# Lambda and the first gate group's rows moved into the input projections of a hybrid attention step

## Chip, cores and metric

One NeuronCore of one Trainium2 chip runs the whole step as one program. The metric is device time in microseconds; several runs are shown by their median. The change is told from no change when it moves the median by more than about 0.5%, which is 13 us here.

## What is computed

One layer for 2048 prompt frames of one stream and 16 new frames of each of 8 running streams (2176 rows in all, width 1024):

```
h   = rms_norm(x, g_in)
qa, ka, va, z_a, qd, ckv, kpe, z_b, m_a, m_b = split(h @ w_in)
lam = exp(sum(lq1*lk1)) - exp(sum(lq2*lk2)) + lam_init
o_a = (softmax(q1 k1) - lam * softmax(q2 k2)) v          # differential attention, 4 heads
o_b = latent attention over rms_norm(ckv) and rope(kpe)    # 4 heads
y_a = W_oa(rms_norm(o_a) * silu(z_a));  y_b = W_ob(o_b * silu(z_b))
out = x + W_out(sigmoid(m_a) * y_a + sigmoid(m_b) * y_b)
```

A final norm follows. `m_a` and `m_b` together are 2048 columns of `w_in`: 16 blocks of 128, called gates here.

## The kernel before

Every matmul of the layer is done in float32 split in two: a value becomes a high part `hi` (a cast on ACT) and a low part `lo` (a subtraction on DVE), and a product is three matmuls, hi·hi, hi·lo and lo·hi (`_mm3`, L97).

The program runs in phases, built by `build` (L1364):

- `_phase_a` (L129): the input projections except the gates, in three parts of rows (`PARTS`), each part 11 pairs of output blocks. Pairs that get a rotation (`rope_pair`, L354) load cosine and sine into the tile `cs`, of which there are two buffers (L360). The normalised rows stand split in `X` (L160); two of these tiles, tags `hi0` and `lo0`, come from the outer pool `zh`.
- `_phase_a2` (L468): queries, keys and values of the latent branch, in six groups of 384 rows (the last has 256). Its results go to DRAM through three rotating buffers (`pair`, L496).
- `_phase_b` (L1006): attention over the prompt, 64 blocks (8 per head and branch; names `d` for differential, `m` for latent). It starts with `_lam` (L660): a product of the four lambda vectors on DVE, one small matmul, an exponential on ACT, two small DVE steps that leave the tile `nlam`.
- `_gates` (L423): the gate columns, in six groups of rows. For one group: the rows are loaded again (four tiles `zx` of two blocks each, from the outer pool `zs`, tag `st`, two buffers), scaled by the norm (L441) and split into `z_hi` and `z_lo` (L442, L443; one buffer each, in the place of `hi0` and `lo0`). Then 16 units follow: load the weight block `zs` (512 KB, the same two `st` buffers), split it into two `zw` tiles (four buffers in all), 24 matmuls of 384 columns into the one PSUM buffer of `zp`, a tanh on ACT (`zt`, L464) and a store to DRAM. Group 1 also writes its split weights to DRAM (`wz`, L458); groups 2 and 5 read these and split nothing.
- `_sample` and `_phase_c`: attention of the 8 running streams, and the output projections.

The order of the instructions is not the order of the code. A scheduler at build time places every instruction on its engine by priority and by its own estimate of when things are ready; groups 0, 1, 2 and 5 of the gates are given the priority of the end of phase A (`prio`, L1374) although their code stands behind phase B, so that their matmuls go wherever TensorE would wait. The engines then run their own lists strictly in order, and the DMA issues of the whole kernel stand in one list, SP's. What the scheduler decided is fixed in the program; on the chip an instruction whose input is late holds up everything behind it on its engine.

Names in the rows: the trace leaves out numbers, so `z` is any gate unit; in the order lists `z1_4` is unit 4 of group 1, `zx0_2` the third row tile of group 0, `zs1_0` a weight block, `sd0_0_...` scores of differential head 0, block 0.

Of the kernel before, what the change touches and what calls it, by code (L numbers as in the profile page):

```python
# [20 lines left out]
P = 128  # L21
# [25 lines left out]
def _consts(c, pool):  # L47
    nc = c.nc
    c.ident = pool.tile([P, P], F32, name="ident")
    make_identity(nc, c.ident)  # L50
    c.ones = pool.tile([P, P], F32, name="ones")
    nc.gpsimd.memset(c.ones, 1.0)
    c.mhalf = pool.tile([P, 64], F32, name="mhalf")
    nc.gpsimd.memset(c.mhalf, -0.5)
    c.vec = pool.tile([P, 20], F32, name="vec")
    nc.sync.dma_start(c.vec, c.i["vec"])
    c.g_in = c.vec[:, 0:8]
    c.g_qa = c.vec[:, 8:12]
    c.g_kva = c.vec[:, 12:14]
    c.gsub = pool.tile([P, 1], F32, name="gsub")  # L60
    nc.vector.tensor_scalar(c.gsub, c.vec[:, 14:15], 1.0 - LAM_INIT, None, op0=ALU.mult)
    c.maskq = pool.tile([P, P], BF16, name="maskq")
    nc.gpsimd.memset(c.maskq, 0.0)
    nc.gpsimd.memset(c.maskq[0:1, 0:64], 1.0)
    c.maskk = pool.tile([P, 64], BF16, name="maskk")
    nc.gpsimd.memset(c.maskk, 0.0)
    nc.gpsimd.memset(c.maskk[0:1, :], NEG)
# [61 lines left out]
def _phase_a(c):  # L129

    nc, tc = c.nc, c.tc
    with (
# [91 lines left out]
        def last_sum(p, raw):  # L224

            n = PARTS[p][1]
            for j in range(4):
                split(raw[j, 1, 0], (z[:, j, n : 2 * n] for z in X[0]))
# [179 lines left out]
        for p in range(len(PARTS)):  # L408
            raw = load_part(p)
            sums(p, raw)  # L410
            v_block(p)
            kpe_block(p)
            last_sum(p, raw)
            for i, f in enumerate(pairs(p)):
                f()
                if p + 1 < len(PARTS):
                    if i < 2 * PARTS[p + 1][1] // P:
                        squares(p + 1, i)
                    elif i == 6:
                        factors(p + 1)  # L420


def _gates(c, prio, g, after, ready):  # L423

    nc, tc = c.nc, c.tc

    def ahead():
        return tc.high_priority(offset=tc.cur_priority - prio)

    t0, n = GROUPS[g]  # L430
    with ahead():
        R = c.zh.tile([P, NG], F32, tag="R", name=f"Rz{g}")[:, :n]
        nc.sync.dma_start(R, c.Rh[:, t0 : t0 + n])
        hi = c.zh.tile([P, KT, NG], F32R, tag="hi0", name=f"z_hi{g}")[:, :, :n]
        lo = c.zh.tile([P, KT, NG], F32R, tag="lo0", name=f"z_lo{g}")[:, :, :n]
        for k2 in range(4):
            x = c.zs.tile([P, 2, NG], F32, tag="st", name=f"zx{g}_{k2}")[:, :, :n]
            nc.sync.dma_start(x, c.i["xT"][:, 2 * k2 : 2 * k2 + 2, t0 : t0 + n])
            for j in range(2):
                k = 2 * k2 + j  # L440
                nc.vector.scalar_tensor_tensor(x[:, j], x[:, j], c.g_in[:, k : k + 1], R, op0=ALU.mult, op1=ALU.mult)  # L441
                nc.scalar.copy(hi[:, k], x[:, j])  # L442
                nc.vector.tensor_tensor(lo[:, k], x[:, j], hi[:, k].bitcast(F32), op=ALU.subtract)  # L443
    for u in range(16):
        nm = f"{g}_{u}"
        with ahead():
            w = [c.zw.tile([P, KT, P], F32R, tag="w", name=f"zw{l}_{nm}") for l in range(2)]
            if ready:
                for l in range(2):
                    nc.sync.dma_start(w[l].bitcast(F32), c.wz[u, l])  # L450
            else:
                st = c.zs.tile([P, KT, P], F32, tag="st", name=f"zs{nm}")
                nc.sync.dma_start(st, c.i["wu"][22 + u])
                for k in range(0, KT, 4):
                    _split(nc, w[0][:, k : k + 4], w[1][:, k : k + 4], st[:, k : k + 4])
                if g == 1:
                    for l in range(2):
                        nc.sync.dma_start(c.wz[u, l], w[l].bitcast(F32))  # L458
        ps = c.zp.tile([P, 512], F32, tag="z", name=f"z{nm}")[:, :n]
        with tc.issue_after(after) if after else nullcontext():  # L460
            _mm3(nc, ps, [(w[0][:, k], w[1][:, k], hi[:, k], lo[:, k]) for k in range(KT)])
        with ahead():
            s = c.zt.tile([P, NG], F32, tag="t", name=f"zt{nm}")[:, :n]
            nc.scalar.activation(s, ps, AF.Tanh, scale=0.5)  # L464
            nc.sync.dma_start(c.smT[u][:, t0 : t0 + n], s)
# [194 lines left out]
def _lam(c, pool, psum):  # L660
# [5 lines left out]
    nc.tensor.matmul(ps[:, 0:2], c.ones, pr, start=True, stop=True)  # L666
    ex = pool.tile([P, 2], F32, name="lam_ex")
    nc.scalar.activation(ex, ps[:, 0:2], AF.Exp)
    c.nlam = pool.tile([P, 1], F32, name="nlam")
    nc.vector.tensor_tensor(c.nlam, ex[:, 1:2], ex[:, 0:1], op=ALU.subtract)  # L670
    nc.vector.tensor_scalar(c.nlam, c.nlam, -LAM_INIT, None, op0=ALU.add)

# [333 lines left out]
def _phase_b(c):  # L1006
    nc, tc = c.nc, c.tc
    GQ = 256
    with (
# [9 lines left out]
        def bank(tag, name):  # L1019
            return pp.tile([P, 512], F32, tag=tag, name=name, bufs={"s": 4, "pt": 2, "o": 1}[tag])  # L1020

        _lam(c, p1, lambda n: bank("o", n))
        onesr = p1.tile([P, 32], F32R, name="onesr")
        nc.scalar.copy(onesr, c.ones[:, :32])
        kp = p1.tile([P, SEQ], F32R, name="kp")
# [338 lines left out]
def build(tc, ins, outs, upto="z", dump=None):  # L1364
# [3 lines left out]
    with tc.tile_pool(name="const", bufs=1) as pool, tc.tile_pool(name="dram", bufs=1, space=DRAM) as dpool:  # L1368
        _consts(c, pool)
        _scratch(c, dpool)  # L1370
        with ExitStack() as stack:
# [3 lines left out]
            _phase_a2(c)  # L1375
            _phase_b(c)
            for g in (0, 1, 2, 5):
                _gates(c, prio, g, None, g in (2, 5))
            _sample(c, stack)
            for g in (3, 4):  # L1380
                _gates(c, prio, g, c.mm.ins, False)
# [95 lines left out]
```

## Time and profile before

| | us |
|---|---|
| three runs: lowest, median, highest | 2585.27, 2591.4, 2596.58 |
| the profiled execution's own time | 2595.66 |
| its span, first to last instruction | 2593.9 |

| engine | busy us | share of the span |
|---|---|---|
| PE (TensorE matmuls) | 2418.1 | 93% |
| DVE (VectorE) | 1645.4 | 63% |
| ACT (ScalarE) | 1224.7 | 47% |
| POOL (GpSimd) | 470.4 | 18% |

The mean granted TensorE clock is 0.975 of full speed. Busy time is a sum over phases with different limits, and a matmul's end is modelled, so short waits of PE do not show in it. The timeline view gives each instruction's start and length, and in brackets the idle time before it and what ended that idle time. SPq rows are DMA issues, not the transfers.

### The profile page before, as it was taken

The numbers are of one execution on the slowest core, as the hardware profiler recorded it, in microseconds if no ns is written. First come the engines' busy times: TensorE is split into PE (matmuls) and PEld (weight loads), VectorE is DVE, ScalarE is ACT, GpSimd is POOL, SyncE is SP. The second block draws the span as 40 slices with busy tenths as digits, with TensorE's granted clock in tenths as the row PEclk, the third lists the DMA queues.
The fourth block names the chain that finished last, engine by engine and source line by source line (L and its number), as shares of the span: only waits on it lengthen the run. The fifth ranks groups of instructions, "written<-read, shape, count | busy, mean of one in ns | idle before, by whom it ended". The sixth has DMA issues, their size and how long they took to land. (4 is left out here: it accounts for less than half of the span.)

```text
span 2593.9 us, 44001 instructions
## 1 busy us (share of the span) xinstructions
PE 2418.1 (93%) x15426; PEld 2149.4 (83%) x15426; DVE 1645.4 (63%) x3668; ACT 1224.7 (47%) x3042; POOL 470.4 (18%) x730
## 2 busy tenths in 40 slices
PE   6998999997899699999999988998999997999998
PEld 5998999997888689899888977887676674988887
DVE  7897686886676477877776688894333223534334
ACT  5544544543444366766665566783334333311111
POOL 0000000000000032333343234443000002122211
PEclk9999999999899899999999999999999998999999
DMA  6977677686687986574666755316869594544332
GB/s 236 306 268 251 210 252 265 204 280 185 228 277 255 299 285 201 183 227 140 182 194 207 232 170 166 92 58 232 325 254 370 222 380 138 174 128 126 121 115 96
DMA packets 303997, 553.28 MB, mean 213 GB/s; under 512 B 29184, under 2 KB 230176, under 8 KB 288544
## 3 DMA queue, kind: packets, MB, share of 16 engines
q1 hardware_dynamic: 303776, 550.46, 64.0%
q8 instruction: 123, 2.02, 0.3%
q14 instruction: 98, 0.80, 0.1%
HBM read 397.16 MB, written 153.19 MB: 212 GB/s over the span
## 5 line engine op out<-in xcount | busy, mean ns | idle before, releaser
L100 PE MATMUL z<-z_hi,zw 128*128 128x384 f32 (+1 forms) x768 | 264.7, 345 | 47.1 <-ACT zt L464 28.2
L102 PE MATMUL z<-z_hi,zw 128*128 128x384 f32 (+1 forms) x768 | 257.9, 336 | 0.4 <-DVE zw L115 0.4
L101 PE MATMUL z<-z_lo,zw 128*128 128x384 f32 (+1 forms) x768 | 258.1, 336 | 0.1
L1079 ACT ACTIVATE ed<-sd,pmd 128x512 f32<-128x512 f32 (+3 forms) x320 | 201.1, 632 | 43.6 <-DVE pmd L1077 23.0
L1077 DVE TENSOR_REDUCE pmd<-sd 128x1 f32<-128x512 f32 (+3 forms) x320 | 189.4, 603 | 49.9 <-PE sd L1178 30.6
L1178 PE MATMUL sd<-k,q 128*128 128x512 f32 (+2 forms) x640 | 193.1, 391 | 13.3 <-ACT ed L1079 8.9
L100 PEld LDWEIGHTS z<-z_hi,zw 128*128 128x128 f32 x768 | 148.6, 193 | 68.6 <-ACT zt L464 36.1
L1118 POOL TENSOR_SCALAR ed<-ed,ad 128x512 f32<-128x512 f32 (+3 forms) x160 | 115.5, 737 | 317.5 <-DVE ad L1094 142.5
L101 PEld LDWEIGHTS z<-z_lo,zw 128*128 128x128 f32 x768 | 148.8, 194 | 7.3 <-issue 4.1
L102 PEld LDWEIGHTS z<-z_hi,zw 128*128 128x128 f32 x768 | 147.9, 193 | 6.5 <-issue 3.4
L109 POOL TENSOR_SCALAR ss<-ss 128x3 f32<-128x3 f32 (+3 forms) x15 | 3.2, 213 | 792.4 <-DVE ss L529 474.1
L115 DVE TENSOR_TENSOR zw<-zs,zw 128x512 fp32r<-128x512 f32 x128 | 84.4, 688 | 92.9 <-ACT zw L114 90.8
L100 PE MATMUL y<-o,wh_ab 128*128 128x384 f32 (+1 forms) x384 | 127.8, 333 | 13.7 <-DVE sm L1303 10.5
L1118 POOL TENSOR_SCALAR em<-em,am 128x512 f32<-128x512 f32 (+3 forms) x160 | 102.9, 660 | 185.5 <-DVE am L1094 115.5
L101 PE MATMUL y<-o,wh_ab 128*128 128x384 f32 (+1 forms) x384 | 126.6, 330 | 0.0
L102 PE MATMUL y<-o,wl_ab 128*128 128x384 f32 (+1 forms) x384 | 126.3, 329 | 0.0
L1178 PEld LDWEIGHTS sd<-k,q 128*128 128x128 f32 x640 | 105.4, 194 | 23.6 <-ACT ed L1079 15.5
L1079 ACT ACTIVATE em<-sm,pmm 128x512 f32<-128x512 f32 (+3 forms) x160 | 100.2, 629 | 47.0 <-DVE pmm L1077 34.2
L1303 DVE SCALAR_TENSOR_TENSOR sm<-sm,y 128x384 f32<-128x384 f32 (+1 forms) x96 | 50.4, 530 | 112.9 <-PE y L102 111.4
L1308 ACT ACTIVATE m<-sm 128x384 fp32r<-128x384 f32 (+1 forms) x48 | 24.3, 506 | 199.0 <-POOL sm L1306 199.0
L1077 DVE TENSOR_REDUCE pmm<-sm 128x1 f32<-128x512 f32 (+3 forms) x160 | 95.6, 603 | 35.3 <-PE sm L1225 27.4
L1135 ACT CAST pthd<-ptd 128x512 fp32r<-128x512 f32 (+3 forms) x160 | 82.6, 522 | 72.1 <-PE ptd L1132 69.6
(521 smaller groups left out, 7579.3 us busy)
## 6 DMA issues: line engine op xcount, KB each, us to landing
zs<-in_wu_dram SPq DMA_DIRECT2D x64, 512.0 KB
zw<-wz SPq DMA_DIRECT2D x64, 512.0 KB
ksd<-in_ckT_dram SPq DMA_DIRECT2D x32, 1024.0 KB
vsd<-in_cv_dram SPq DMA_DIRECT2D x32, 1024.0 KB
q<-Qs SPq DMA_DIRECT2D x128, 128.0 KB
wz<-zw SPq DMA_DIRECT2D x32, 512.0 KB
ksm<-in_cc_dram SPq DMA_DIRECT2D x16, 1024.0 KB
smT<-zt SPq DMA_DIRECT2D x80, 192.0 KB
```

The lines of the kernel that those rows point to most:

```text
L100: nc.tensor.matmul(out, ah, bh, start=(j == 0), stop=False)
L101: nc.tensor.matmul(out, ah, bl, start=False, stop=False)
L102: last = nc.tensor.matmul(out, al, bh, start=False, stop=(j == n - 1))
L109: c.nc.gpsimd.tensor_scalar(ss, ss, scale, EPS, op0=ALU.mult, op1=ALU.add)
L115: nc.vector.tensor_tensor(lo, src, hi.bitcast(F32), op=ALU.subtract)
L1077: nc.vector.tensor_reduce(nm_, ps[:, :w], axis=AX.X, op=ALU.max, negate=True)
L1079: nc.scalar.activation(e[:, :w], ps[:, :w], AF.Exp, bias=nm_, accum_out=l[:, s, i : i + 1])
L1118: nc.gpsimd.tensor_scalar(p, p, a[:, 0, j : j + 1], 1.0, op0=ALU.mult, op1=ALU.mult)
L1135: nc.scalar.copy(hi, v)
L1178: nc.tensor.matmul(ps[:, :n], qs[s][:, j, qc], ks[s].tiles[i][:, :n], start=(j == 0), stop=(j == 1 and not last))
L1303: nc.vector.scalar_tensor_tensor(s, s, 1.0, ps, op0=ALU.add, op1=ALU.mult)
L1308: nc.scalar.mul(z[0], sm[0], 0.5)
```

## The change

Three edits. The lambda steps run in phase A, in part 0, after the block `kpe_block`, with a PSUM bank of phase A; `nlam` moves to the constant pool. The rows of gate group 0 are loaded and split by a new function, `_gate_rows`, called at the end of phase A's code, and their four `zx` tiles come from the two `cs` buffers of the rotation tables instead of the two `st` buffers. The other groups call the same function with the `st` buffers, as before.

```diff
+            if p == 0:
+                _lam(c, pc, bank)
...
+        c.rows = _gate_rows(c, 0, lambda name: pc.tile([P, 2, NG], F32, tag="cs", name=name, bufs=2))
+
+
+def _gate_rows(c, g, get):
...
+    for k2 in range(4):
+        x = get(f"zx{g}_{k2}")[:, :, :n]
+        nc.sync.dma_start(x, c.i["xT"][:, 2 * k2 : 2 * k2 + 2, t0 : t0 + n])
+        for j in range(2):
+            k = 2 * k2 + j
+            nc.vector.scalar_tensor_tensor(x[:, j], x[:, j], c.g_in[:, k : k + 1], R, op0=ALU.mult, op1=ALU.mult)
+            nc.scalar.copy(hi[:, k], x[:, j])
+            nc.vector.tensor_tensor(lo[:, k], x[:, j], hi[:, k].bitcast(F32), op=ALU.subtract)
+    return hi, lo
...
-def _gates(c, prio, g, after, ready):
+def _gates(c, prio, g, after, ready, rows=None):
...
-        for k2 in range(4):
-            x = c.zs.tile([P, 2, NG], F32, tag="st", name=f"zx{g}_{k2}")[:, :, :n]
...
+    if rows is None:
+        with ahead():
+            rows = _gate_rows(c, g, lambda name: c.zs.tile([P, 2, NG], F32, tag="st", name=name))
+    hi, lo = rows
...
-    c.nlam = pool.tile([P, 1], F32, name="nlam")
...
-        _lam(c, p1, lambda n: bank("o", n))
...
-                _gates(c, prio, g, None, g in (2, 5))
+                _gates(c, prio, g, None, g in (2, 5), c.rows if g == 0 else None)
```

Both programs hold the same number of instructions on every engine. What differs is where they stand.

SP's list at the end of phase A. `qdT`, `ckT` and `gzT` are stores of phase A; `ws_uq` and `qd0` are loads of phase A2. Before:

```order
L438 DMA zx0_2_19654<-in_xT_dram 128x2x384
L438 DMA zx0_3_19662<-in_xT_dram 128x2x384
L385 DMA ckT_84<-m1l12_2_6477 128x320
L481 DMA ws_uq0_6606<-in_wuq_dram 128x512
L385 DMA ckT_84<-wl12_2_6480 128x320
L433 DMA Rz1_20246<-Rh_94 128x384
L385 DMA ckT_84<-vl12_2_6478 128x320
L453 DMA zs0_0_19672<-in_wu_dram 128x1024
L385 DMA ckT_84<-u3l12_2_6479 128x320
L481 DMA ws_uq1_6612<-in_wuq_dram 128x512
L453 DMA zs0_1_19708<-in_wu_dram 128x1024
L509 DMA qd0_6656<-qdT_83 128x4x384
```

And of the change, the same stretch:

```order
L386 DMA qdT_84<-u3l10_2_6354 128x320
L467 DMA zs0_2_19744<-in_wu_dram 128x1024
L437 DMA zx0_2_6613<-in_xT_dram 128x2x384
L437 DMA zx0_3_6621<-in_xT_dram 128x2x384
L386 DMA ckT_85<-m1l12_2_6486 128x320
L495 DMA ws_uq0_6651<-in_wuq_dram 128x512
L386 DMA ckT_85<-wl12_2_6489 128x320
L467 DMA zs0_3_19780<-in_wu_dram 128x1024
```

The weight blocks of units 0 and 1 (`zs0_0`, `zs0_1`) now stand 31 and 19 issues earlier, among phase A's last stores; here unit 2's comes ahead of the third and fourth row tiles, which keep their place.

ACT's list at the border of phases A2 and B. `kz5` and `z_hi1` are splits, `onesr` a constant of phase B, `ed0_0` the first exponentials of attention. Before:

```order
L442 CAST z_hi1_20248<-zx1_2_20266 128x384 x2
L1024 CAST onesr_8364<-ones_65 128x32
L442 CAST z_hi1_20248<-zx1_3_20274 128x384 x2
L668 ACT_TABLE_LOAD
L668 ACTIVATE lam_ex_8359<-lam_ps_8357 128x2
L114 CAST zw0_1_0_20282<-zs1_0_20284 128x512 x2
L114 CAST zw0_1_1_20320<-zs1_1_20322 128x512 x2
L464 ACTIVATE zt1_0_20317<-z1_0_20292 128x384
L1079 ACTIVATE ed0_0_0_0_0_8399,ld0_0_0_8389<-sd0_0_0_0_0_8394,pmd0_0_0_8388 128x128
```

And of the change:

```order
L602 CAST kz5_8370<-kp5_8360 64x256
L478 ACTIVATE zt1_9_20659<-z1_9_20634 128x384
L115 CAST zw0_1_11_20700<-zs1_11_20702 128x512 x2
L478 ACTIVATE zt1_10_20697<-z1_10_20672 128x384
L115 CAST zw0_1_12_20738<-zs1_12_20740 128x512 x2
L478 ACTIVATE zt1_11_20735<-z1_11_20710 128x384
L1036 CAST onesr_8400<-ones_65 128x32
L478 ACTIVATE zt1_12_20773<-z1_12_20748 128x384
L115 CAST zw0_1_13_20776<-zs1_13_20778 128x512 x2
L115 CAST zw0_1_14_20814<-zs1_14_20816 128x512 x2
L478 ACTIVATE zt1_13_20811<-z1_13_20786 128x384
L478 ACTIVATE zt1_14_20849<-z1_14_20824 128x384
```

The next two rows of the change are the table load and `ed0_0`. Before, the first exponentials of attention come behind unit 0 of group 1; now behind unit 14. PE's list agrees: ahead of the first score `sd0_0` stood unit 0 alone, now units 0 to 14, of which 0 to 2 and the start of 3 lie among the last matmuls of phase A2, and 4 to 14 follow each other with no other matmul between.

SP's list at the same border, of the change (before, `kp<-Kp` and the first `q` stood ahead of `zs1_0`):

```order
L467 DMA zs1_13_20778<-in_wu_dram 128x1024
L472 DMA wz_96<-zw1_1_11_20701 128x1024
L472 DMA wz_96<-zw0_1_12_20738 128x1024
L479 DMA smT_88<-zt1_11_20735 128x384
L467 DMA zs1_14_20816<-in_wu_dram 128x1024
L472 DMA wz_96<-zw1_1_12_20739 128x1024
L1038 DMA kp_8402<-Kp_92 128x2048
L1066 DMA q0_0_0_8404<-Qs_80 64x2x256
L1067 DMA q0_0_0_8404<-Qs_80 64x2x256
```

The loads for the first attention blocks now stand behind the weight block of unit 14. With 14 units less to spread, the last unit of group 5 on PE moves from block d2_5/m2_2 of attention forward to about d2_2/m2_5.

## Rows read from the trace of the kernel before

**Rows 1.** The page's first part: busy us, share of the span, instructions.

```profile
PE 2418.1 (93%) x15426; PEld 2149.4 (83%) x15426; DVE 1645.4 (63%) x3668; ACT 1224.7 (47%) x3042; POOL 470.4 (18%) x730
```

**Rows 2.** Windows: stretch, length, busy us by engine, PEclk, DMA share, GB/s.

```profile
620.90:640.00 19.10, 7.16 (x27) 6.62 (x28) 11.43 (x21) 8.13 (x14) 0.00 (x0) 0.73 0.88 266
700.00:862.50 162.50, 152.86 (x862) 146.85 (x860) 110.24 (x233) 71.18 (x146) 8.24 (x17) 0.97 0.84 269
862.50:888.00 25.50, 6.85 (x29) 6.41 (x28) 10.61 (x23) 8.99 (x19) 1.27 (x3) 0.60 0.87 266
```

**Rows 3.** Timeline of PE, first gate units: start us, length us, instruction, idle before.

```profile
631.77 0.69 PE L100 MATMUL z<-z_hi,zw 128*128 128x384 f32 x1 [10.89 <-ACT zw L114]
...
649.38 0.44 PE L100 MATMUL z<-z_hi,zw 128*128 128x384 f32 x1 [4.19 <-ACT zt L464]
...
650.05 0.52 PE L100 MATMUL z<-z_hi,zw 128*128 128x384 f32 x1
...
657.04 0.44 PE L100 MATMUL z<-z_hi,zw 128*128 128x384 f32 x1 [0.96 <-ACT zt L464]
...
661.14 0.34 PE L102 MATMUL z<-z_hi,zw 128*128 128x384 f32 x1
665.97 0.69 PE L100 MATMUL z<-z_hi,zw 128*128 128x384 f32 x1 [4.49 <-ACT zt L464]
```

**Rows 4.** Timeline of ACT, DVE and SP, the rows and first weights of group 0.

```profile
615.64 1.76 ACT L442 CAST z_hi<-zx 128x384 fp32r<-128x384 f32 x4 [4.81 <-PE p4l L324]
...
617.24 1.72 SPq L438 DMA_DIRECT2D zx<-in_xT_dram  x2
...
621.07 1.15 DVE L441 SCALAR_TENSOR_TENSOR zx<-zx,vec,Rz 128x384 f32<-128x384 f32 x2 [1.42 <-DMA zx<-in_xT_dram]
...
625.48 0.36 SPq L453 DMA_DIRECT2D zs<-in_wu_dram  x1
...
626.32 1.02 DVE L443 TENSOR_TENSOR z_lo<-zx,z_hi 128x384 fp32r<-128x384 f32 x2
...
631.11 1.14 ACT L114 CAST zw<-zs 128x512 fp32r<-128x512 f32 x2 [5.49 <-DMA zs<-in_wu_dram]
```

**Rows 5.** Timeline at the border of phases A2 and B.

```profile
873.70 1.28 ACT L668 ACT_TABLE_LOAD   x1
...
873.83 0.58 PE L666 MATMUL lam_ps<-lam_pr,ones 128*128 128x2 f32 x2 [11.21 <-DVE lam_pr L664]
874.57 0.53 SPq L453 DMA_DIRECT2D zs<-in_wu_dram  x1
...
881.19 1.14 ACT L114 CAST zw<-zs 128x512 fp32r<-128x512 f32 x2 [6.02 <-DMA zs<-in_wu_dram]
...
881.86 0.69 PE L100 MATMUL z<-z_hi,zw 128*128 128x384 f32 x1 [7.45 <-ACT zw L114]
```

**Rows 6.** Windows of the tanh line alone, by head: length, busy us (count), PEclk, DMA share, GB/s.

```profile
888.00:1152.63 264.63, 9.82 (x20) 0.99 0.73 237
1152.63:1381.68 229.05, 6.71 (x14) 0.99 0.60 180
...
1607.69:1778.46 170.77, 0.00 (x0) 0.96 0.26 76
```

**Rows 7.** Timeline of ACT, the tanh of the first three units of group 1.

```profile
888.02 0.49 ACT L464 ACTIVATE zt<-z 128x384 f32<-128x384 f32 x1 [3.72 <-PE z L102]
...
893.88 0.49 ACT L464 ACTIVATE zt<-z 128x384 f32<-128x384 f32 x1 [1.44 <-PE z L102]
...
900.51 0.49 ACT L464 ACTIVATE zt<-z 128x384 f32<-128x384 f32 x1 [0.22 <-PE z L102]
```

**Rows 8.** Windows, two stretches of the highest transfer rate; columns as in rows 2.

```profile
885.00:890.00 5.00, 5.00 (x33) 4.82 (x33) 1.63 (x7) 1.83 (x8) 0.01 (x1) 0.95 1.07 372
890.00:895.00 5.00, 4.78 (x28) 4.37 (x27) 2.92 (x8) 2.86 (x9) 1.27 (x3) 1.00 1.03 415
```

**Rows 9.** Timeline of PE, first score and first transpose of attention.

```profile
887.82 0.40 PE L1178 MATMUL sd<-k,q 128*128 128x256 f32 x2
...
893.68 0.49 PE L1132 MATMUL ptd<-ident,ed 128*128 128x128 f32 x3
```

More of the change, by code (lines that the diff above doesn't have):

```diff
@@ L61, in _consts @@
     nc.vector.tensor_scalar(c.gsub, c.vec[:, 14:15], 1.0 - LAM_INIT, None, op0=ALU.mult)
+    c.nlam = pool.tile([P, 1], F32, name="nlam")
     c.maskq = pool.tile([P, P], BF16, name="maskq")
@@ L420, in _phase_a @@
                         factors(p + 1)
-def _gates(c, prio, g, after, ready):
+        c.rows = _gate_rows(c, 0, lambda name: pc.tile([P, 2, NG], F32, tag="cs", name=name, bufs=2))
+def _gate_rows(c, g, get):
+    nc = c.nc
+    t0, n = GROUPS[g]
+    R = c.zh.tile([P, NG], F32, tag="R", name=f"Rz{g}")[:, :n]
+    nc.sync.dma_start(R, c.Rh[:, t0 : t0 + n])
+    hi = c.zh.tile([P, KT, NG], F32R, tag="hi0", name=f"z_hi{g}")[:, :, :n]
+    lo = c.zh.tile([P, KT, NG], F32R, tag="lo0", name=f"z_lo{g}")[:, :, :n]
+    for k2 in range(4):
[8 more added lines that the diff above has]
+def _gates(c, prio, g, after, ready, rows=None):
     nc, tc = c.nc, c.tc
@@ L430, in _gates @@
     t0, n = GROUPS[g]
[L431 to L435, printed above, removed]
-        for k2 in range(4):
-            x = c.zs.tile([P, 2, NG], F32, tag="st", name=f"zx{g}_{k2}")[:, :, :n]
[L438 to L443, printed above, removed]
+    if rows is None:
+        with ahead():
+            rows = _gate_rows(c, g, lambda name: c.zs.tile([P, 2, NG], F32, tag="st", name=name))
+    hi, lo = rows
     for u in range(16):
```

## The prediction

> **What bounds the kernel now.** I read the first part of the page first: PE is busy 2418 of 2594 us, no other engine above 63% [rows 1]. So the time is what PE has to do plus what it waits for, and since both programs hold the same instructions, only the waits, the clock and the overlap can change. I then looked, in the windows, for stretches in which PE is idle around the places that the change touches. There are two: at the end of phase A PE works 7.2 of 19.1 us, at the border of A2 and B 6.9 of 25.5 us, while inside A2 it works 153 of 162.5 us [rows 2]. Next comes the timeline of these stretches, to see what each idle time waits for. The first (10.89 us) ends with the cast of a weight block `zw` [rows 3]. Ahead of it ACT, DVE and SP show the row tiles arriving one after the other, and the weight block issued only at 625.48, when a `st` buffer was free [rows 4]. The second is two waits, 11.21 us for lambda's product on DVE and 7.45 us for `zw` again [rows 5]. At the border the weight block was issued at 874.57 and its cast began at 6.62 us after that; so even without lambda unit 0 of group 1 could not have started much before 881 there. Last I read by head what attention costs with and without gate units [rows 6].
>
> **The price of a unit.** The clean one starts at 657.04, its last matmul starts at 661.14: 4.10 us for 23 steps, 0.178 each, so 24 matmuls are 4.28 us, here 4.3. With one PSUM buffer the next unit waits for the tanh: 0.96 us of idle at best, so that units in a row cannot follow closer than 4.44 + 0.96 = 5.4 us [rows 3].
>
> **Part 1, start of the gates after phase A.** Removed: the two `st` buffers no longer carry row tiles, so weight blocks 0 and 1 are loaded during phase A, 31 and 19 issues earlier on SP. Not removed: four row tiles still share two buffers. The third and fourth are issued where they were, at 617.24, and reach DVE at 621.07; the last split seen there is two subtractions from 626.32 to 627.34 [rows 4]. PE could begin with the first rows' products when the last projection ends, 620.9, and finish unit 0 when the last rows are split, with a few matmuls left: about 629. Before, 24 steps from 631.77 under a half clock (0.69 us a matmul, 0.73 granted over the stretch [rows 2, 3]) end at about 638.3, an estimate. That is 9; unit 1 follows at the bank's pace, which gives back part, so I take **−7.5**. Ends: −4, where the clock still falls during the remaining waits, and −10, no more than the idle time itself is 10.9.
>
> **Part 2, the border.** Lambda goes to phase A: DVE's product, PE's 0.58 us, ACT's two steps. DVE and ACT are not the bound in phase A, which I take from their shares [rows 1]; PE's own 0.58 us stays, **+0.6** (0 to 2, the upper end if its wait on DVE shows, since PE's list is strict). The units of group 1 now reach into the tail of A2, so lambda's 11.2 us and `zw`'s 7.45 us both lose their cause: **−18.7**. The near end, −14, leaves room for one late first block of weights in A2 (an idle of 4.19 or 4.49 us, as seen twice at the first gates [rows 3]).
>
> **Part 3, eleven units with nothing between them.** This is what the change adds. Before, PE did units 1 to 14 of group 1 between the products of attention; now 4 to 14 stand alone ahead of the first score. A unit inside attention costs its 4.3 us and no more: head 1 takes 229.05 us with 14 units, of which 12 are full and two of the short last group at 2.9 (256 of 384 columns); less 12 × 4.3 + 2 × 2.9 = 57.4 it is 171.7, and the head without units takes 170.77 [rows 6]. So in leaving attention each unit returns 4.3 us and costs its pace P in the row: 11 × (P − 4.3). P is at least the 5.4 of the bank. The other limit is traffic: a unit of group 1 loads 512 KB, writes 1024 KB of split weights and 192 KB of results, 1.77 MB. At the 372 and 415 GB/s of the busiest stretches [rows 8] that is 4.8 and 4.3 us; at 266, the rate of the border now [rows 2], 6.7 us. The weight blocks of units 4 on have both `st` buffers from the start, so the loads run ahead, and I take P = 5.6, just above the bank's pace: **+14.3**. Ends: 5.4 (+12.1) and 7.0 (+29.7), the upper one between the traffic at 266 GB/s and the 7.7 us from 649.38 to 657.04 at the first gates [rows 3].
>
> **Part 4, the tail of A2.** Units 0 to 2 and the start of 3 run between A2's last matmuls, where DMA is already at a share of 0.84 [rows 2]. Three times 1.77 MB at 372 GB/s are 14 us of transfers that A2's own loads and stores have to share. In 162.5 us at 0.84 the free share is 26 us, so most fits: **+3**, between 0 and 8.
>
> **Part 5, the first softmax.** Before, unit 1 lay between the first score at 887.82 and the first transpose at 893.68, and covered the exponentials [rows 9]. Now nothing of the gates stands there, and the exponential table's 1.28 us load [rows 5] moves onto this chain. The chain is 5.86 us, of which the other scores fill about 1.4 (an estimate: three more of 0.40): **+4.5**, ends 2 and 8. The first attention loads are now issued behind weight block 14, but that block is wanted some 10 us before the first score, so they should be in time.
>
> **Part 6, filler missing later.** The gate units now end three pairs of blocks earlier in the third head. Attention without them is no slower than with them, net of their 4.3 us [rows 6]: **0**.
>
> **The sum.** −7.5 + 0.6 − 18.7 + 14.3 + 3 + 4.5 = −3.8 us. The 1.8 us around the span stay. Against the profiled execution (2595.7) this gives 2591.9; that execution was 4.3 above the median of the runs, so against the median it is 2587.6, **2588**. This is no measurable change: a difference under 0.5%, 13 us, cannot be told from none here. All ends together would reach from −35 to +34, but they do not fall on one side together.
>
> **Rivals.**
> *It gains more than I allow (faster).* The row of units runs at the bank's 5.4, the start gives its full 10, A2's tail costs nothing, the softmax chain 2, and head 0 loses its crowding: now it takes 264.63 us with 19 units [rows 6], 182.9 without them, 11 more than head 1; with most units gone it could give back 9. Sum: −10 + 0.6 − 18.7 + 12.1 + 0 + 2 − 9 = −23, 2568. For it: DMA share 1.00 and above in that head's start [rows 8]. Against: part of head 0's surplus may be the start of attention itself. It decides from 9 us below my sum on.
>
> *The row of units is paced by its weights (slower).* Each unit needs load, split on ACT and DVE, matmuls, and then a write of its split weights ahead of the next loads in SP's one list. Where this chain is not run ahead, units follow at 7.7 and 8.9 us [rows 3] and tanhs of group 1 at 5.86 and 6.63 [rows 7]. At P = 8: 11 × 2.4 = 26.4 above my sum, +22.6, 2614. It is slower than the bound from P = 7.1 on, that is when DMA gives less than 250 GB/s. Against it: the first gates were late because row tiles held the buffers, and at B's start DMA gave 372.
>
> *The rows gain nothing (same).* The two `cs` buffers hold row tiles 2 and 3 back just as the two `st` buffers did, and SP issues them where it did [rows 4]; if PE's first unit must wait for these anyway, the −7.5 is 0 and the sum +3.7, 2595.
>
> *The clock falls in the row of units (slower).* In the trace, matmuls after 0.96 us of idle are still 0.44 and then 0.34 us long, after 4.19 us of idle 0.52, and after 10.89 us 0.69 [rows 3]: only the longer idles go with the half clock, 1.2 GHz, and a row with 1.1 to 1.3 us between units should stay at 2.4 GHz. If instead the clock were low in half of the eleven units, each of these would take twice its 4.28 us of matmuls: 5.5 × 4.28 = 23.5 above my sum, +19.7, 2611. The Trainium skill, "TensorE: Matmul & The Clock Gate", section "A second HAM failure mode: psum-queue depth-cycling", describes this case: short idles between groups of matmuls, as PSUM buffers are cycled, make the clock swing between its two levels. By that rule this rival would hold; the trace so far does not agree with it after 0.96 us.
>
> **Chances and range.** My sum 0.5; gains more 0.2; paced by weights 0.15; rows gain nothing 0.1; clock 0.05. So faster 0.2, same 0.6, slower 0.2. The range runs from 2573, which takes in most of the ends of the start, the tail and head 0, to 2608, which is P = 7.4; 0.1 is left out at each end, the clock's case among it.
>
> **What would show it.** Right: the first gate matmul at about 621 and unit 1 at about 633; no idle of 11 and 7 us at the border; tanhs of units 4 to 14 some 5.6 us apart with a granted clock near 1; the first transpose about 4.5 us of idle after the scores; heads without units at 171 us. Wrong: tanhs over 7 us apart, PE waiting for `zw` between them, an idle of over 4 us before the first score (its loads late), or PE in A2's tail waiting for `qd` loads.

## The result, and the profile after

The changed kernel takes 2606.52 us (median of 5 runs, 2603.97 to 2607.36), the kernel before in the same comparison 2592.12: ratio 1.0054, interval 1.0041 to 1.0067, 14.4 us slower. The forecast was 2588, no measurable change. The profiled execution of the changed kernel has a span of 2605.6 us, with PE busy for 2440.1 us of it (94%).

At the two places that I had looked at, the long idle times are gone, as forecast. Timeline of PE after, first gate units, beside [rows 3]:

```profile
624.83 0.34 PE L101 MATMUL z<-z_hi,zw 128*128 128x384 f32 x1
...
628.27 0.44 PE L102 MATMUL z<-z_lo,zw 128*128 128x384 f32 x1 [1.02 <-DVE z_lo L442]
...
631.66 0.69 PE L102 MATMUL z<-z_lo,zw 128*128 128x384 f32 x1 [0.29 <-DVE z_lo L442]
...
636.34 0.69 PE L101 MATMUL z<-z_hi,zw 128*128 128x384 f32 x1 [2.71 <-ACT zt L478]
```

The idle 10.89 us are gone: unit 0 starts as phase A ends and waits about a microsecond at a time for its last rows. Next the row of units 4 to 14 ahead of the first score. Timeline of ACT after, the tanhs of units 3, 4 and 14, beside [rows 7]:

```profile
874.99 0.49 ACT L478 ACTIVATE zt<-z 128x384 f32<-128x384 f32 x1 [1.69 <-PE z L103]
880.55 0.49 ACT L478 ACTIVATE zt<-z 128x384 f32<-128x384 f32 x1 [2.64 <-PE z L103]
...
933.87 0.49 ACT L478 ACTIVATE zt<-z 128x384 f32<-128x384 f32 x1 [4.52 <-PE z L103]
```

From the tanh of unit 3 to that of unit 14 are 58.88 us: eleven units at 5.35 each, under my 5.6. PE after, the shortest and the longest idle between two of them:

```profile
881.09 0.44 PE L101 MATMUL z<-z_hi,zw 128*128 128x384 f32 x1 [0.58 <-ACT zt L478]
...
886.10 0.44 PE L101 MATMUL z<-z_hi,zw 128*128 128x384 f32 x1 [0.58 <-ACT zt L478]
...
908.46 0.44 PE L101 MATMUL z<-z_hi,zw 128*128 128x384 f32 x1 [1.10 <-ACT zt L478]
```

Windows of the changed kernel, columns as in [rows 2]. The three stretches are A2, the row of units, and the opening, that is the start of attention behind the row:

```profile
700.00:862.50 162.50, 152.90 (x849) 146.57 (x848) 112.50 (x234) 74.30 (x150) 8.36 (x16) 0.96 0.87 280
875.90:934.00 58.10, 49.78 (x266) 45.20 (x265) 15.93 (x29) 18.57 (x41) 1.18 (x4) 1.00 1.04 371
934.00:980.00 46.00, 36.48 (x159) 28.23 (x160) 24.90 (x61) 21.47 (x60) 9.72 (x15) 0.85 1.03 342
```

The kernel before, 46 us from its first score on:

```profile
887.80:934.00 46.20, 43.49 (x240) 37.85 (x239) 25.57 (x64) 24.65 (x69) 11.45 (x21) 1.00 1.00 355
```

Here is the first loss. In the opening PE is idle for 9.5 us, before for 2.7, and the granted clock is 0.85, before 1.00. In the 46 us from the first score on stand 1.5 gate units, before 4.7. What PE waits for there, timeline after, beside [rows 9]:

```profile
935.53 0.48 PE L1190 MATMUL sd<-k,q 128*128 128x256 f32 x2 [1.70 <-DMA v<-Vs]
939.76 0.97 PE L1144 MATMUL ptd<-ident,ed 128*128 128x128 f32 x3 [2.40 <-POOL ed L1135]
...
954.79 0.47 PE L1233 MATMUL sm<-kn,qn 128*128 128x512 f32 x1 [0.94 <-DMA kn<-Kn]
...
965.46 0.50 PE L1233 MATMUL sm<-kn,qn 128*128 128x512 f32 x1 [1.35 <-ACT em L1091]
```

By the timeline some 4.5 of the 9.5 us end with an attention load (1.5 ahead of the first score, 3.0 in five waits for `kn`), 3.75 with the exponentials (the 2.40 above and 1.35 in the latent branch), the rest mostly with a gate unit's weights.

The second loss is some 850 us later, in the sample phase (the attention of the running streams), which no edit touches. `ssd` are the scores of its first stream, `Wsd` their weights after the softmax, `atsd` the transposes of these. PE after, then PE in a second trace of the kernel before:

```profile
1804.14 1.06 PE L836 MATMUL ssd<-ksd,sp 128*32 128x512 f32 x8
1808.49 7.09 PE L858 MATMUL atsd<-Wsd,esd 128*128 128x64 f32 x32 [3.29 <-DVE Wsd L853]
```

```profile
1794.65 1.92 PE L823 MATMUL ssd<-ksd,sp 128*32 128x512 f32 x16
...
1800.78 3.68 PE L845 MATMUL atsd<-Wsd,esd 128*128 128x64 f32 x32
```

Before, a gate unit stands between these two rows and covers the softmax. After, none does: PE idles 3.29 us, and the same 32 matmuls take 7.09 us, before 3.68; the granted clock over them is 0.50 (1.2 GHz), before 1.00 (2.4 GHz).

**All stages.** The start of the same matmul differs between two traces also by the gate units done until then, which are the same work at another time. So I take 4.28 us off for each (two thirds of that for the short ones of group 5); what is left is called net of units. The table gives it by stage, in us: the mean of three traces with the order of before, and of five whose order is the changed kernel's up to the sample phase (for the last two stages, two traces of each kernel itself). "om" and "y" are the last products of attention and the first of the output projection; the mark in the middle of attention is the matmul that starts at 1436 us in the kernel before:

| stage, to | forecast | before | changed | difference |
|---|---|---|---|---|
| phase A | +0.6 | 620.6 | 622.1 | +1.5 |
| start of the gates, first qn of A2 | -7.5 | 31.7 | 24.9 | -6.9 |
| A2, last qp | +3 | 135.1 | 136.1 | +1.0 |
| border, first score | -4.4 | 26.7 | 16.9 | -9.7 |
| opening, middle of the first heads | +4.5 | 57.3 | 72.9 | +15.6 |
| attention, until the mark at 1436 | 0 | 339.4 | 331.4 | -7.9 |
| attention's end, last om | 0 | 311.8 | 323.9 | +12.1 |
| sample, first y | 0 | 273.1 | 280.6 | +7.5 |
| output, a late y | 0 | 382.3 | 383.5 | +1.2 |

The sum is +14.4, as is the difference of the medians. The border and the opening go together, since a unit done in the one is missing in the other: they come to +5.9. The three traces of before lie within 3.8 us of each other in every stage, the five of the change within 4.8.

### The profile page after: what moved, and what is told of

Read it like the earlier page. It is cut to its first block, busy times and chain, and to the rows that moved or that the text cites. A ratio compares the mean times of both kernels' runs of the same rounds, so it can differ in the third digit from the quotient of the medians.

```text
span 2605.6 us, 43991 instructions
## 1 busy us (share of the span) xinstructions
PE 2440.1 (94%) x15426; PEld 2156.1 (83%) x15426; DVE 1643.1 (63%) x3668; ACT 1223.5 (47%) x3042; POOL 464.1 (18%) x730
## 5 line engine op out<-in xcount | busy, mean ns | idle before, releaser
L1148 DVE TENSOR_TENSOR ptld<-ptd,pthd 128x512 fp32r<-128x512 f32 (+3 forms) x160 | 95.4, 601 | 33.8 <-ACT pthd L1147 33.3
```

The costliest lines, as they stand in the source:

```text
L1148: nc.vector.tensor_tensor(ptl[ch][:, :n, i * P : (i + 1) * P], v, hi.bitcast(F32), op=ALU.subtract)
```

## The experiments

Each ran against the kernel before in five rounds. "Sample" is the time from the last om to the first y, units included, in that run's trace, which is a single execution.

| run | median us | ratio, interval | sample |
|---|---|---|---|
| before_again | 2591.18 | 0.9994 (0.9985 to 1.0002) | 408 |
| after_again | 2603.67 | 1.0042 (1.0030 to 1.0054) | 416 |
| lam_only | 2599.42 | 1.0030 (1.0018 to 1.0042) | 419 |
| rows_only | 2592.03 | 0.9997 (0.9985 to 1.0009) | 413 |
| after_sample | 2606.66 | 1.0059 (1.0043 to 1.0076) | 418 |
| before_gap | 2603.18 | 1.0034 (1.0022 to 1.0046) | 423 |
| after_hold | 2599.94 | 1.0028 (1.0019 to 1.0038) | 420 |
| hold_sample | 2607.42 | 1.0059 (1.0045 to 1.0073) | 429 |
| after_rsub | 2606.51 | 1.0049 (1.0031 to 1.0068) | 418 |
| after_rsub_unit | 2603.25 | 1.0036 (1.0023 to 1.0048) | 421 |
| h5_l2 | 2593.49 | 1.0001 (0.9990 to 1.0011) | 415 |
| h6_l1 | 2602.16 | 1.0030 (1.0016 to 1.0044) | 419 |
| open_p1 | 2601.68 | 1.0048 (1.0028 to 1.0067) | 424 |
| rows_p1 | 2587.33 | 0.9984 (0.9974 to 0.9994) | 413 |
| rows_h5_l2 | 2587.73 | 0.9984 (0.9971 to 0.9997) | 412 |
| rows_h4_l1 | 2578.63 | 0.9954 (0.9936 to 0.9972) | 407 |
| after_pair6 | 2575.26 | 0.9951 (0.9937 to 0.9964) | 421 |
| before_pair6 | 2566.54 | 0.9912 (0.9898 to 0.9925) | 410 |

**1. The same programs again, and each edit alone.**

> The kernel before, unchanged, once more: a ratio of 1.000, and a second trace that tells how far two executions of one program differ from place to place. If the 4.1 us that phase A was longer in the changed kernel's trace is mostly the luck of DMA (0.97 us before the first matmul, 2.6 us at a projection that waits for a weight block), then this trace too should move by 1 to 3 us at those places. If it is the change, phase A here ends within 0.5 us of 620.9.

> The changed kernel, unchanged, once more: 1.0054 within 0.001. In its trace the start of the gates should again be some 8 us earlier against phase A's end, the units of group 1 follow at 5.3 to 5.4 us, and the sample phase be some 7 us longer than before, with an idle of about 3.3 us and matmuls at half clock ahead of its first atsd. If the sample's loss was an accident of one execution, it is missing here.

> Lambda alone moved to phase A; the rows of group 0 as before. In its order only unit 0 of group 1 stands ahead of the first score, so there is no row of units; and in the sample phase no gate unit stands between the last ssd0 and the first atsd, as in the changed kernel. Theory A (the units and the border balance, and the loss comes from knock-on order in the sample phase): the border is shorter by 8 to 15 us, the sample phase longer by 6 to 11 us, sum -8 to 0, about 2588. Theory B (the loss comes from the row of units and the border): no row, no loss, 2591 - 11 to 19 = 2573 to 2580.

> The rows of group 0 through the cs tiles, lambda left in phase B. The row of units stands as in the changed kernel (4 to 12, lambda, 13, 14), but in the sample phase a gate unit stands between the last ssd0 and the first atsd, as before. Theory A: start -8, border 0 to +4, end of the gate units in attention +6, sample 0: 2588 to 2594, at least 8 below the changed kernel. Theory B: the whole loss is here, 2600 to 2608.

The second trace of before has phase A 2.4 us longer than the first, so most of the 4.1 us by which the changed kernel's first trace was longer there was luck; five traces of the change give +1.5. Lambda alone (the lines of the diff on `_lam` and `nlam`) costs some 7 us. The rows alone (those on `_gate_rows`) cost nothing in all, though their trace has the change's long opening (72.4 us): the start of the gates, 10.0 us shorter, goes against it. Added to the rows, lambda costs 11.6 us in the medians. With lambda alone the border does not get shorter at all (26.8 us net of units). Timeline of PE, lam_only:

```profile
877.16 0.69 PE L101 MATMUL z<-z_hi,zw 128*128 128x384 f32 x1 [19.33 <-ACT zw L115]
```

The two waits of [rows 5], 11.21 and 7.45 us, have become one of 19.33. In the one trace of lam_only the sample phase is 9.1 us longer, and no other stage more than 1.4. But that trace is of its fastest run (2587.67), 12 us under its median and no slower than before in all; so it does not show where the usual run loses its 7. The median, 2599, is above both theories' ranges, the traced run inside A's.

**2. The order in the sample phase.**

`c.at` holds instructions by name, and the matmuls of a unit may not stand ahead of the one named. The line that matters of both edits, the second for before_gap, the third for after_sample (the lines that record the instructions and pass them on are left out):

```diff
-                _gates(c, prio, g, c.mm.ins, False)
+                _gates(c, prio, g, lambda u: c.at["posd0"] if g == 3 and u == 4 else c.mm.ins, False)
+                _gates(c, prio, g, lambda u: c.at["ssd0_3"] if g == 3 and u == 3 else c.mm.ins, False)
```

> The mirror image: the kernel before, with unit 4 of group 3 held back until the first posd of the sample phase, so that no unit stands between the last ssd0 and the first atsd. If the order costs what the traces say: an idle of about 3.3 us there, atsd at half clock, 3 to 8 us slower than before: 2596 to 2601. If the loss in the sample phase has another cause: 2590 to 2594.

> The changed kernel, with one gate unit of the sample phase (unit 3 of group 3) held back until the last ssd0 has been issued, so that it stands ahead of the first atsd as before; what follows it in the sample phase is placed anew by the scheduler. If the knock-on order is what the sample phase lost: no idle of 3.3 us ahead of atsd, no half clock behind it, the stretch from the last om to the first otsm 10 us shorter, and, as the rest of the phase gave 4 to 7 us of it back, 4 to 10 us in all: 2595 to 2601. If that idle only moves to another place of the phase: 2603 to 2607.

Timeline of PE, before_gap:

```profile
1800.92 5.27 PE L846 MATMUL atsd<-Wsd,esd 128*128 128x64 f32 x32 [3.29 <-DVE Wsd L841]
```

The kernel before, changed in nothing but the place of one unit (and what the scheduler puts behind it), has the same idle of 3.29 us and is 9 to 11 us slower (by the ratio and by the medians). In its trace only the sample phase is longer, by 13.3 us; every other stage is within 1.2 us of before. The way back failed: after_sample has no idle ahead of atsd, but one of 6.0 us ahead of otsd, a transpose of the first stream's result. There POOL is late. Timeline of POOL after, then in the second trace of before:

```profile
1810.79 1.31 POOL L110 TENSOR_SCALAR rsub<-rsub 128x8 f32<-128x8 f32 x5 [30.19 <-DMA rsub<-rsub]
...
1826.80 0.55 POOL L111 TENSOR_TENSOR v1sd<-v0sd,mhalf 128x1 f32<-128x1 f32 x1
```

```profile
1780.39 1.32 POOL L109 TENSOR_SCALAR rsub<-rsub 128x8 f32<-128x8 f32 x5 [7.68 <-DMA rsub<-rsub]
```

The row sums' load stands 17.5 us later on SP, behind eight loads of cached keys and values, and POOL's 16 us of work on them stand ahead of the first stream's norm. So the load was put back in its old place, alone (after_rsub) and together with the unit of after_sample (after_rsub_unit):

```diff
-            nc.sync.dma_start(ss, flat)
+            with c.tc.high_priority(offset=c.tc.cur_priority - c.rsub_at):
+                nc.sync.dma_start(ss, flat)
```

> The changed kernel with one load moved: the row sums of the first branch (rsub), which POOL turns into factors at the start of the sample phase, are issued on SP ahead of the cached keys and values again, as before the change (they had slid behind eight loads of 1 MB, from 2.8 us after the last om to 20.4). POOL works 16 us on them ahead of the first stream's norm in its fixed order. Expected: POOL begins near 8 us instead of 30.6 after the last om, otsd waits for no one; the idle of 3.3 us ahead of atsd stays, since no gate unit stands there. If the late load is the larger part of what the sample phase lost: 2597 to 2601; if the missing unit ahead of atsd is: 2602 to 2606.

> The same load moved, and unit 3 of group 3 held back behind the last ssd0 as well, so that both marks of the order before are restored: the unit ahead of atsd, and POOL's work done in time for otsd. If these two make the sample phase's loss, the phase takes 409 to 413 us as in the three traces with the old order, and the time is 2594 to 2600; what is left above the kernel before is then the border's and attention's. If the phase still takes 416 to 420: 2602 to 2607, and the cause in it is a third one.

The load alone gives nothing. Both together mend the first stream (first otsm, a transpose of the second branch, 95.2 us after the last om, 96 to 97 before, 110 to 112 in the change), but the rest of the phase loses it again: 421 us in all. So taking the unit away from this one place is shown to cost time (before_gap), but putting it back does not return it; which of the later places take the time is not settled. Over all runs the phase goes with the order: the seven traces in which the scheduler itself put a whole unit between the last ssd and the first atsd (with the first trace of before, 412) take 407 to 413 us; the thirteen others (with the first of the change, 419) take 415 to 429, five of them with a unit held there by hand and lam_only with the last third of one.

**3. The row of units.** The edit of after_hold; hold_sample adds that of after_sample:

```diff
-                _gates(c, prio, g, None, g in (2, 5), c.rows if g == 0 else None)
+                _gates(c, prio, g, lambda u: c.at["sd0"] if g == 1 and u > 3 else None, g in (2, 5), c.rows if g == 0 else None)
```

> The changed kernel without the row of units: units 4 and up of group 1 may be issued only behind the first score of attention. In its order unit 4 follows that score at once and the units are spread over attention almost as before (the last at d2_5). If the row is what the border and the end of the gate units lose: PE waits 5 to 8 us for the first attention loads instead of doing eleven units, the border is 6 to 14 us shorter net of units, and attention from the third head on loses nothing for want of units; 2589 to 2598, the sample phase still long. If a row at 5.35 us is as good a filler as any: 2602 to 2610, since PE now waits.

> Both together, no row of units and the unit of the sample phase held back: if both losses are separate and as large as thought, the sum of the two gains against the changed kernel, 2582 to 2592, no slower than before and perhaps 5 us faster. If they are not, about what the better of the two alone gives.

PE, after_hold:

```profile
903.57 0.76 PE L1191 MATMUL sd<-k,q 128*128 128x256 f32 x2 [29.66 <-DMA k<-Ks]
```

Without the row PE waits 29.66 us for the first keys, not 5 to 8. Border and opening together are 92 us net of units, with the row 89.8, before 84.0: the row is as good a filler as any. What it fills is a wait that the change made longer: the cast of A2's last keys (`kz`, see 5) comes 17.4 us behind A2's last matmul here, 6.6 before. The time, 2599.9, lies between the two forecasts. What after_hold gains on the change (4 to 7 us) stands in attention's end, +3.5 where the change has +12.1: 2.0 units are missing there instead of 6.7. hold_sample lost in the sample phase (429 us) what it should have gained.

In the next two the number 3 became 4 and 5, and the sample phase has the edits of after_rsub_unit. The priority for the weights, stores and tanhs of group 1 is lowered to that of the end of A2, from unit 2 on in h5_l2 (the edit shown) and from unit 1 on in h6_l1:

```diff
-        return tc.high_priority(offset=tc.cur_priority - prio)
+        return tc.high_priority(offset=tc.cur_priority - (c.prio_b if g == 1 and u >= 2 else prio))
```

> Both marks of the sample phase restored, and the row of units cut: units 5 and up of group 1 only behind the first score, and the weights, stores and tanhs of units 2 and up at a lower priority than phase A2, so that the stores of A2's last keys and the first attention loads are not queued behind split weights. Two units (3 and 4) stand between A2 and the first score. In the kernel with the row held back alone PE waited 29.7 us there for the first keys, since SP issued A2's last store 18 us after its matmuls. If the queue ahead of those stores is what made that wait: a wait under 12 us here, the end of the gate units later again, 2584 to 2594. If the wait is the loads' own time: 18 us or more, 2594 to 2604.

> As the one before with one unit more ahead of the first score (3 to 5) and the lower priority from unit 1 on: 5 us less wait for the first keys, 5 us more of units. 2584 to 2594 if the queue is the cause, and within 3 us of the one before; if the wait is the loads' own time, some 4 us faster than the one before.

The wait was 26.93 us in h5_l2 and 25.25 in h6_l1, so a lower priority for the units' transfers did not shorten it much. In h5_l2 the wait fits the second theory (18 us or more) and the time the first (2584 to 2594), so neither holds as a whole; h6_l1, 9 us slower than h5_l2, is outside both. h5_l2 came back to the time of before by attention's end (8.2 us shorter than in the change). h6_l1 has lost most of that again (6.2 us longer there than h5_l2, 3.8 longer in the sample phase); why is open.

**4. The opening, and lambda left in its place.** The edit of open_p1; rows_p1 is rows_only with the same lines:

```diff
+            prio1 = tc.cur_priority
             _phase_b(c)
...
-                _gates(c, prio, g, None, g in (2, 5), c.rows if g == 0 else None)
+                _gates(c, prio1 if g == 1 else prio, g, None, g in (2, 5), c.rows if g == 0 else None)
```

> The changed kernel with one number changed: the weights, stores and tanhs of gate group 1 get the priority of the end of phase A2 instead of phase A's. In its order the row is two units shorter, and units 13 and 14 stand behind the first scores, ahead of the first transpose, where before the change unit 1 stood; the sample phase's order stays the changed kernel's. If the opening of attention (from the first score on, 15 us longer net of units than before in two traces) lost for want of units there, it gets 5 to 10 us shorter and the time is 2595 to 2601. If it lost to the transfers queued there, which stay: 2602 to 2607.

> The same one number in the kernel with the rows edit alone (lambda in phase B, the sample phase's order as before): the same gain on 2592, if it is one: 2584 to 2589, and else 2590 to 2595.

The opening is 7.8 us shorter in open_p1 than in the change, and 1.8 shorter in rows_p1 than in rows_only; of the 7.8 the border takes 3 back. So units there help, by 2 to 5 us net, and the rest of the loss stays. open_p1's time shows no gain, its sample phase took 424 us; rows_p1 gains 5 on rows_only. All twenty traces fit this: the opening's length, net of units, goes with the units that stand in its first 46 us. With 3.7 to 4.7 of them it is 56 to 58 us, with 2.5 (open_p1) 65, with 1.5 to 2.0 it is 71 to 73.

The last two of this set are rows_only with the edits of h5_l2 on group 1, and the same with one unit less and the lower priority from unit 1 on.

> The row cut after unit 4 and the lower priority from unit 2 on, as in the kernel that came back to the time of before, but with lambda left in phase B, where it now stands behind unit 4 ahead of the first score, in the wait for the first keys. Its sample phase has the order of before, with no unit held there. If moving lambda costs through the sample phase alone: that phase 408 to 413 us instead of 415, 2587 to 2591, a little under before. If lambda's wait on DVE shows again at the border: 2593 to 2603.

> As the one before with one unit less ahead of the first score and the lower priority from unit 1 on. Within 4 us of it if the wait for the first keys is set by the queue, as its end then does not hang on the units in front.

rows_h5_l2 differs from h5_l2 by lambda's place and the sample phase's order. It is 5.8 us faster in the median, inside the range for a cost through the sample phase alone; but that phase gives only 3 of it (412 us for 415), so "alone" is not shown. rows_h4_l1 beats both kernels, at 2578.6: 9 us under rows_h5_l2, where at most 4 were expected; its border is no shorter (33.6 us for 33.8 net of units), the gain is in attention (7.3) and the sample phase (4.9), and not explained.

**5. What sets the border.** ACT, kernel before and after: what it waits for behind A2's last matmul, and the cast of A2's last result (`kz`). The first attention load, `kp`, needs the store of `kz`:

```profile
860.54 0.28 ACT L503 ACTIVATE knz<-kn 128x128 fp32r<-128x128 f32 x1 [1.44 <-DMA Qn<-qnz]
...
866.39 0.41 ACT L588 CAST kz<-kp 64x256 fp32r<-64x256 f32 x1
```

```profile
890.57 0.49 ACT L478 ACTIVATE zt<-z 128x384 f32<-128x384 f32 x1 [3.91 <-PE z L103]
...
907.63 0.39 ACT L602 CAST kz<-kp 64x256 fp32r<-64x256 f32 x1
```

PE's last A2 matmul starts at 859.8 and 875.9. ACT needs 7 and 32 us to write what is left. In the kernel before it waits for the stores that free the three buffers, 0.4 to 1.4 us at a time. In the changed kernel it mostly waits for the matmuls of the row's units, 2 to 4 us at a time, because their tanhs stand ahead of A2's casts in its list. I then gave A2's results six buffers:

```diff
-            return pn.tile([P, 2, 512], F32, tag="hl", name=name, bufs=3)[:, :, :n]
+            return pn.tile([P, 2, 512], F32, tag="hl", name=name, bufs=6)[:, :, :n]
```

> The changed kernel with six rotating buffers for A2's results instead of three (line 510). In the kernels so far ACT writes A2's last results one by one, each waiting for an earlier result's store to land and, in its fixed order, behind gate units' casts and tanhs; Kp's cast stands at 866.4 in the trace of before, 883.8 in the best kernel, 907.6 in the changed one, and the first keys can only be loaded after it. If this drain sets the border, then six buffers shorten it: in its order no row of units is left, only three units stand there, the first score comes within 25 us of A2's last matmul, border and opening together lose the 6 us they cost above before and 5 to 15 more; 2585 to 2598, with the sample phase still long. If the attention loads' own time sets it: 2600 to 2608.

> The kernel before with the same six buffers, which leaves lambda in phase B and the old sample order. If the drain also made lambda's wait of 11.2 us (its product stands on DVE behind A2's last results), that wait falls under 4 us here without moving lambda: 2570 to 2585. If lambda's wait has another cause, it stays: 2588 to 2594.

With six buffers kz stands 2 us behind A2's last matmul in both, the first score follows that matmul at 17.8 us, and lambda's wait is gone without moving lambda. Both times are under the ranges that I had given. The gains, 28 us on after_again and 24 on before, are the largest of the study. PE, before_pair6, the longest wait left at the border:

```profile
849.32 0.79 PE L1178 MATMUL sd<-k,q 128*128 128x256 f32 x2 [2.11 <-DMA k<-Ks]
```

By stage the gain is not where I looked for it. In the trace of before_pair6 (19.4 us shorter than the mean of before) the border is 15.5 us shorter, but the opening 14.7 longer, so that the two together give 0.8; A2 itself gives 9.4, attention 4.6, phase A and the start 4.2. The opening is as long there as in the change (71.9 us, before 57.3), with a granted clock of 0.82, although the kernel has none of the change's edits: 2.0 units stand in its first 46 us, before 4.7. The scheduler's order is new here too, so the buffers' own share is not separated from that of the order.

The change is still 8.7 us slower than its counterpart, with 421 us against 410 in the sample phase.

## Why the prediction was wrong

The sum of the forecast was -3.8 and the stages give +14.4. Of the 18.2 us between them the sample phase has 7.5, border and opening together 5.8, the rest of attention 4.2, and the other stages 0.7.

**Phase A and the start: right.** +0.6 and -7.5 against +1.5 and -6.9. **A2's tail**, +3 against +1.0, was inside its bounds.

**The border: better than forecast, the opening far worse.** -4.4 against -9.7: units at 5.35 us instead of 5.6 make 2.8 of the 5.3 us between them, the rest I have not traced. The 5.4 that units "cannot follow closer than" was no floor: two starts above are 5.01 us apart. But +4.5 for the opening, ends 2 and 8, measured +15.6. The step that failed was "Before, unit 1 lay between the first score ... and covered the exponentials": I priced one softmax, while units 1 to 4 and most of 5 had stood in the first 46 us of the opening, beside its exponentials and the waits for `kn`. Without them PE idles 9.5 us, and the clock falls with it (0.85). The sentence on the loads, "so they should be in time", was wrong too: the first score waited 1.70 us for an attention load, and about half of the opening's idle time ends with such loads. Over all traces the opening is long where units are missing in it, in before_pair6 too, which has none of the change's edits.

**Part 6, "Attention without them is no slower than with them", measured +4.2**, as -7.9 and +12.1. I took two heads for all. Near the end a unit partly fills time that PE would idle: 6.7 units fewer there returned 6.7 × 4.28 - 12.1 = 16.6 us, 2.5 each and not 4.28. Between the opening and the mark at 1436, 3.9 units fewer returned 7.9 us more than their 4.28 each, as the rival on head 0 had said. These prices are worked out from the stage table; no experiment varied the units of these stretches alone.

**The sample phase: no term at all, +7.5.** The step that failed is the first paragraph's: "I then looked ... around the places that the change touches". The scheduler places every instruction anew, and both orders were there to be compared to the end. What the runs show instead: with one unit moved in that phase, and none of the change's edits, the kernel before is 9 to 11 us slower (before_gap). The same omission hides lambda's price: "PE's own 0.58 us" is right for its instructions, and moving it cost some 7. That the part of these 7 behind attention comes from the order is likely, as the phase is long wherever the order is the new one; how much of them it is stays open.

**The rivals.** The slower one (row paced by its weights, P from 7.1) is refuted: P was 5.35. That the rows gain nothing at the start of the gates is refuted too (-6.9). The clock in the row: in the window of the row the granted clock is 1.00 with 0.58 to 1.10 us between units. That speaks against the rule in the Trainium skill, "TensorE: Matmul & The Clock Gate", section "A second HAM failure mode: psum-queue depth-cycling", for idles as short as these. The granted clock fell behind the row, where idles of 1.70 and 2.40 us followed each other. No rival named the mechanism that came. The sentence on all ends together is wrong as a sum: the ends as written add up to -15 and +30, not -35 and +34.

**Beneath it** lay a wrong reading of [rows 5], that both waits there "lose their cause". DVE, kernel before:

```profile
870.90 2.24 DVE L441 SCALAR_TENSOR_TENSOR zx<-zx,vec,Rz 128x384 f32<-128x384 f32 x4 [3.32 <-DMA zx<-in_xT_dram]
...
873.62 0.15 DVE L664 TENSOR_TENSOR lam_pr<-vec 128x2 f32<-128x2 f32 x1
```

Lambda's product was late because it stood on DVE behind the last row tiles of group 1. Those were late because their two buffers were freed by splits that stand on ACT and DVE behind A2's last results, and these waited for the stores of earlier results. Taking lambda's wait away alone moved it to the weights (lam_only); taking both away put the row's units and their casts ahead of A2's last results. With six buffers for these results (before_pair6) lambda's wait is gone and the kernel is 24 us faster, though most of the gain lies outside border and opening.

## What to carry to other kernels

Where a scheduler places instructions, compare the two orders over the whole program, on every queue, before a forecast, and give each stretch whose order moved a term or a doubt. Price a filler (work that can go anywhere, like the gate units) by the stretch that it leaves: taking it out returns its own time only where the engine would otherwise be busy. Follow a wait that names a small step (a product on DVE) back to what that step is queued behind, here row tiles, casts and in the end three buffers, before moving the step. And after a fix, look by stage for where the gain lies: six buffers were meant for the border, and most of their gain was elsewhere.

## What was not expected of the hardware

Behind an idle of 3.28 or 3.29 us on PE the next 32 matmuls took 7.09 us in five traces, 5.68 and 5.27 in two more (granted clock 0.50, 0.64 and 0.69), and 3.68 at a clock of 1.00 in the twelve traces without an idle there. So an uncovered wait of that length cost 1.5 to 2 times itself. In lam_only an idle of 1.67 us was enough for 5.84 us (0.62). Why the same idle costs more in one trace than in another is not shown. Executions of the kernel before lie between 2582.1 and 2599.8 us over all sets of runs, and the two traces of it differ by 10.5 us, in no stage by more than 3.8: so a difference of a few us between two single traces says nothing here, and the main table compares several of each. Stage figures of the experiments rest on one trace each.
